# Shorter inverse roots, mixer B's key and value tiles in banks of three tags, and its first head four filling steps later

## The chip, the cores and the metric

The kernel runs on one core of one Trainium2 chip. The metric is the device time of one execution in microseconds (us). In the profile PE is the matrix engine (TensorE), PEld its weight loads, DVE the vector engine (VectorE), ACT the scalar engine (ScalarE), POOL is GpSimd, and SP is the engine that issues most of the DMAs (SyncE). A matmul's result goes to one of eight PSUM banks of 128 × 512 numbers.

## What is computed

Two layers of a trunk over 512 positions of width 1024, in float32. Each layer has two attention mixers side by side, gates that merge them, and then a channel mixer. Cut to what matters here:

```
h = rms_norm(x)
z = h @ W_in                # columns for mixer A, for its indexer, for mixer B, for two gates
# mixer A: indexer scores, the 128 best keys of each query (top-k), attention over these, 8 heads
# mixer B: latents, 8 heads of 64 + 32 numbers
cq   = rms_norm(cq);  qb = cq @ w_uq     # 384 -> 8 x 96, rotary on the last 32
ckv  = rms_norm(ckv); kv = ckv @ w_ukv   # 256 -> 8 x (64 key + 64 value)
kb   = concat(kv[..., :64], rope(kr))    # kr: 32 numbers that all heads share
qb, kb = rms_norm(qb), rms_norm(kb)      # over the 96 numbers of a head
y_b  = softmax(mask(qb @ kb.T * scale)) @ kv[..., 64:]
x = x + (sigmoid(ga) * (y_a @ w_a) + sigmoid(gb) * (y_b @ w_b)) @ w_out
x = x + down(silu(gate) * val)           # [gate, val] = conv3(rms_norm(x) @ w_up)
```

Every rms_norm needs an inverse square root of a mean of squares per position (or per position and head).

## The kernel before, in words

**Products.** [...] A product is then three matmuls: high × high, high × low, low × high. ScalarE copies out the high part, VectorE subtracts it from the source to make the low part (`split_into`, lines 312–319: the low part is due one tick after the high part). For weights the same is done ahead of their use (`Weights.split`), for some of them by a DMA that adds on GpSimd's queue (line 211).

**Order of the work.** The program is written as generators. `mix_dense` (line 572 on) is the *filling*: the dense columns of the input projection (line 535), mixer B's key, value and query tiles, mixer A's query, key and value rows (line 558). One filling step is the work up to its next `yield`: for dense columns three matmuls of 512 columns. A `Feeder` called `each_b` goes between the steps of mixer B's heads, and each call gives 0.85 filling steps while the first two heads run (`RATE_B`), and 0.2 steps of the top-k. The top-k (`top_k`, lines 1036 and 1043) is VectorE work: sixteen rounds of three maxima and three match-replaces over 512, 384 and 256 columns. It is handed out between filling steps, one operation per step while mixer B's first group of heads is made (`RATE_0`, line 1258). `later(n, f)` puts off `f` by n ticks. From what is so written the scheduler of the framework makes a fixed order of the instructions of each engine; each engine then runs its own queue in that order and waits at its head for whatever the instruction needs.

**PSUM.** The eight banks are handed out by tag: two of D (dense), three of L, two of T (mostly transposes), one of Y (line 277). A new tile of a tag takes the bank of the tile that many of its tag before, and its first matmul waits until that one's readers are done.

**Mixer B's tiles.** `attn_b(g)` (from line 833 on) makes heads 4g to 4g + 3. For each of the four blocks of 128 positions a key/value tile is made: six matmuls of 512 columns (line 856). Its bank is read by ScalarE (line 862, keys into `kn`; line 314, the values' high part into `vb`; line 843, squares into `sqb`) and by VectorE (line 315, the values' low part); line 844 sums the squares on VectorE into `ssk`. Three ticks later `keys()` adds to them the sum of squares of the shared rotary key `sskr` (line 870), makes the mean (line 871), the inverse root, and 22 ticks later scales the keys (`kn`, lines 879–880 on VectorE, the rotary part on GpSimd). Then four query tiles: nine matmuls of 384 columns each (line 893); ScalarE copies them out into `qn` (line 899), GpSimd turns them (lines 906–912), and `queries()` scales them (line 924, VectorE). All of these tiles have tag L (`BB`, line 97).

**The heads.** Before mixer B's first head `each_b` is called `GAP_B` = 12 times (line 1290). `turn_b` transposes a head's queries and keys (line 1149, into banks T) and splits them, `scores_b` makes its four rows of scores (lines 1164–1166, three matmuls each in a bank L), VectorE takes the maxima, ScalarE the exponentials (line 369), `softmax_end` scales them (lines 1056–1063), and `values` transposes the weights (line 1074) and multiplies (line 1081, bank Y). The scores of a head, the values of the head before and the transposes of the next go in turn, with `each_b` between.

**The inverse root** (`rsqrt`, line 343) is on VectorE: a first guess from the bits (line 346) and three Newton steps of three operations (lines 355–357), ten in a chain, on 4 or 16 numbers per partition. It is used by `Norm.finish` (line 485, then a copy in line 486), for the latents, for mixer A's heads, and in `keys()` and `queries()`.

Of the kernel before, what the change touches and what calls it, by code (L numbers as in the profile page):

```python
# [15 lines left out]
OP = mybir.AluOpType  # L16
AX = mybir.AxisListType
# [7 lines left out]
EPS = 1e-6  # L25
# [17 lines left out]
RATE_T = 0.2  # L43
LAG_S = 22
LAG_T = 4
GAP_B = 12
NORM_ACT = [3]
E_V = [2, 1, 2, 2, 2, 0]
PT = 0
# [29 lines left out]
LAG_D = [2, 4, 5, 7, 8, 10, 12]  # L79
WPOOL = []  # L80
WMOD = 1
NEWT = 1
WB = [4, 4, 3]
ENDS = 20
SPARE = (1, 3, 5)
# [9 lines left out]
GAP_I = 4  # L95
GAP_A = 12
BB = 'L'
LAG_N = 16
LAG_Q = 6
PSUM = {'D': 2, 'L': 3, 'T': 2, 'Y': 1}  # L100
# [146 lines left out]
def trunk(ctx: ExitStack, tc: tile.TileContext, xT, wd, vecs, bias, rot_n, outT):  # L247
# [92 lines left out]
        mm(p, lhsT=ah, rhs=bl, start=False, stop=False, skip_group_check=True)  # L340
        mm(p, lhsT=al, rhs=bh, start=False, stop=stop, skip_group_check=True)

    def rsqrt(a, shape, quick=False):

        y, t = small("y", shape), small("t", shape)
        V.tensor_scalar(y.bitcast(I32), a.bitcast(I32), -0.5, float(0x5F3759DF), op0=OP.mult, op1=OP.add)
        if not (quick or NEWT):
            for _ in range(3):
                G.tensor_tensor(out=t, in0=y, in1=y, op=OP.mult)
                G.tensor_tensor(out=t, in0=t, in1=a, op=OP.mult)  # L350
                G.tensor_scalar(t, t, -0.5, 1.5, op0=OP.mult, op1=OP.add)
                G.tensor_tensor(out=y, in0=y, in1=t, op=OP.mult)
            return y
        for _ in range(3):
            V.tensor_tensor(out=t, in0=y, in1=y, op=OP.mult)
            V.scalar_tensor_tensor(t, t, -0.5, a, op0=OP.mult, op1=OP.mult)
            V.scalar_tensor_tensor(y, t, 1.5, y, op0=OP.add, op1=OP.mult)
        return y

    def pin(ins, i, k):  # L360
        if i == 0 and k in PINS:
# [89 lines left out]
    class Norm:  # L451
# [17 lines left out]
        def finish(self, gap, turned):  # L469

            p = bank("T")
            v = small("v", [4])
            for i in range(4):
                c = slice(i * 128, (i + 1) * 128)
                if turned:
                    pin(nc.tensor.transpose(p[:, c], self.acc[:, c], ident), i, "F")
                else:
                    pin(mm(p[:, i:i + 1], lhsT=self.acc[:, c], rhs=ones[:, 0:1], start=True, stop=True), i, "F")
            if turned:
                V.tensor_reduce(out=v, in_=p.rearrange("p (t c) -> p t c", c=128), axis=AX.X, op=OP.add)  # L480
            total = v if turned else p[:, 0:4]
            self.epsv = cst.tile([128, 4], F32, name=nm("epsv"))
            self.rstd = cst.tile([128, 4], F32, name=nm("rstd"))
            V.tensor_scalar(v, total, 1.0 / D, EPS, op0=OP.mult, op1=OP.add)
            r = rsqrt(v, [4], quick=True)
            V.tensor_copy(self.rstd, r)
            V.tensor_scalar(self.epsv, v, EPS, None, op0=OP.mult)
            self.row = slot("row")

            def rest():  # L490
                self.spread(self.rstd, self.row)
                for f in self.waiting:
                    f()
                self.waiting = None
            later(gap, rest)
# [72 lines left out]
    st = {}  # L568
# [3 lines left out]
    def mix_dense(l, nrm):  # L572
# [23 lines left out]
        def turn_wk(wk):  # L596
# [33 lines left out]
            G.tensor_tensor(out=k3, in0=k3, in1=nrm.rstd[:, :, None].to_broadcast([128, 4, 32]), op=OP.mult)  # L630
            G.tensor_tensor(out=t3, in0=k3, in1=k3, op=OP.mult)
            ss = cst.tile([128, 4], F32, name=nm("sskr"))
            later(6, lambda: V.tensor_reduce(out=ss, in_=t3, axis=AX.X, op=OP.add))
            st["kr"], st["sskr"] = k3, ss

        raw, sqs = [], []
# [196 lines left out]
        def attn_b(g):  # L833
# [14 lines left out]
            h, o = W.get("kv", g)  # L848
            for t in range(4):
                ts = slice(t * 128, (t + 1) * 128)  # L850
                p = bank(BB)
                xs = [(st["ckvh"][k][:, ts], st["ckvl"][k][:, ts]) for k in range(2)]
                seq = ([(x, h, k) for k in range(2) for x in xs[k]] + [(xs[k][0], o, k) for k in range(2)] if "k" in LO
                       else [q for k in range(2) for q in ((xs[k][0], h, k), (xs[k][1], h, k), (xs[k][0], o, k))])
# [12 lines left out]

            def keys():
                m = small("mk", [4, 4])
                V.tensor_tensor(out=m, in0=ssk, in1=st["sskr"][:, :, None].to_broadcast([128, 4, 4]), op=OP.add)  # L870
                V.tensor_scalar(m, m, 1.0 / 96, EPS, op0=OP.mult, op1=OP.add)
                r = rsqrt(m, [4, 4])

                def scale():
# [776 lines left out]
```

## Time and profile before

| | |
|---|---|
| time, median of 3 runs | 1536.77 us (1535.88 to 1537.1) |
| the profiled execution | 1536.24 us, span 1534.5 us from its first to its last instruction |
| granted TensorE clock | 1.00 of full speed over the whole span |
| TensorE busy | 1525.7 us |
| VectorE busy | 1124.4 us |
| ScalarE busy | 946.3 us |
| GpSimd busy | 396.3 us |
| mixer B's key, value and query tiles and first heads | about 90 to 136 us in layer 0, 853 to 900 us in layer 1 |

A row of the time line is: start in us, duration in us, engine, line, operation, the tile written and the tiles read (numbers left out), for a matmul its rows and columns, then partitions × elements; in brackets how long the engine was idle before it and what ended that. Durations of one engine's instructions overlap: the next starts before the last part of the one before is written, so what one costs its queue is the distance of starts, which the prediction uses.

### The profile page before, as it was taken

Reading aid. Unit: us, or ns where it says so; the run is one execution under the profiler, and the core shown is the slowest. Engines: PE = TensorE matmul, PEld = TensorE weight load, DVE = VectorE, ACT = ScalarE, POOL = GpSimd, SP = SyncE. Lnnn points to the kernel's source line nnn. Section 1 sums busy time; section 2 is a strip of 40 time slices with the busy share of each in tenths; the row PEclk is TensorE's granted clock in tenths of the full one; section 3 lists DMA queues with packets and bytes.
Section 4 is the critical chain, followed back from the end, with each engine's and each line's share of the span. In section 5 each row is a group of like instructions: output and inputs, shape, how many; then the busy total and the mean of one; then the engine's idle time right before and its main releaser. Section 6 shows DMA issues by size and latency. Waiting matters only on the chain.

```text
span 1534.5 us, 23946 instructions
## 1 busy us (share of the span) xinstructions
PE 1525.7 (99%) x8658; PEld 1335.7 (87%) x8658; DVE 1124.4 (73%) x2305; ACT 946.3 (62%) x1553; POOL 396.3 (26%) x578
## 2 busy tenths in 40 slices
PE   9999999999999999999999999999999999999999
PEld 8887999888888898889998889998888888988899
DVE  7899988666476693547979999886674857835586
ACT  7756668773577536664557576687635765456642
POOL 2343012400011442124602520223001115311364
PEclk9999999999999999999999999999999999999999
DMA  7464124733488438873454641356436783488732
GB/s 247 108 158 119 53 86 113 190 118 116 128 191 190 104 117 218 194 177 90 152 171 112 159 107 56 104 134 174 129 97 147 182 189 91 149 197 197 181 99 91
DMA packets 73575, 216.29 MB, mean 141 GB/s; under 512 B 8432, under 2 KB 11504, under 8 KB 73456
## 3 DMA queue, kind: packets, MB, share of 16 engines
q1 hardware_dynamic: 54592, 149.08, 30.7%
q0 software_dynamic: 18432, 65.28, 22.8%
q8 instruction: 68, 1.11, 0.3%
q14 instruction: 51, 0.42, 0.1%
q10 hardware_dynamic: 432, 0.40, 0.1%
HBM read 141.06 MB, written 4.19 MB: 95 GB/s over the span
## 4 chain that ended last, share of the span: by engine, by line
PE 86%; DVE 11%; ACT 2%; issue 1%; DMA 0%; SPq 0%; DVEq 0%; ACTq 0%
PE D L535 37%; PE T L535 15%; PE D L558 7%; PE L L1446 5%; PE T L1446 4%; PE D L1446 3%; DVE sc L1043 2%; PE Y L1081 2%; DVE m L1036 2%; PE Y L1446 2%; PE T L1074 2%; PE L L535 2%; PE L L336 1%; PE L L335 1%; PE L L728 1%
## 5 line engine op out<-in xcount | busy, mean ns | idle before, releaser
L182 ACT CAST wh<-wr 128x1024 fp32r<-128x1024 f32 (+2 forms) x205 | 211.3, 1034 | 163.7 <-PE D L535 73.8
L211 POOL DMA_DIRECT2D wl<-wr x128 | 110.7, 874 | 630.2 <-ACT wl L210 591.9
L535 PE MATMUL D<-hxh,wh 128*128 128x512 f32 (+1 forms) x440 | 174.0, 396 | 0.0
L535 PE MATMUL D<-hxl,wh 128*128 128x512 f32 (+1 forms) x440 | 172.8, 393 | 0.0
L210 ACT ACTIVATE wl<-wr 128x1024 fp32r<-128x1024 f32 (+2 forms) x128 | 132.2, 1035 | 48.1 <-PE D L535 25.9
L200 ACT CAST wh<-wr 128x896 fp32r<-128x896 f32 x88 | 82.6, 942 | 102.4 <-POOL wr L224 56.2
L1115 POOL TENSOR_TENSOR P<-M,sel 128x128 f32<-128x128 f32 (+1 forms) x64 | 53.4, 889 | 271.2 <-DMA M<-in_bias_dram 150.2
L535 PE MATMUL D<-hxh,wl 128*128 128x512 f32 (+1 forms) x440 | 117.8, 393 | 0.0
L224 POOL TENSOR_TENSOR wr<-wr 128x256 f32<-128x256 f32 x88 | 101.0, 1151 | 57.9 <-DVE wr L223 41.9
L558 PE MATMUL D<-wh,hxh 128*128 128x256 f32 x384 | 113.8, 297 | 0.0
L205 DVE TENSOR_TENSOR wl<-wr,wh 128x896 fp32r<-128x896 f32 x88 | 101.9, 1161 | 10.2 <-ACT wh L200 4.3
L558 PE MATMUL D<-wl,hxh 128*128 128x256 f32 x384 | 109.3, 285 | 0.0
L558 PE MATMUL D<-wh,hxl 128*128 128x256 f32 x384 | 108.4, 283 | 0.0
L535 PE MATMUL D<-hrl,wh 128*128 128x512 f32 x256 | 99.6, 389 | 0.0
L535 PE MATMUL D<-hrh,wh 128*128 128x512 f32 x256 | 99.6, 389 | 0.0
L535 PE MATMUL T<-hrh,wh 128*128 128x512 f32 x256 | 99.6, 389 | 0.0
L535 PE MATMUL T<-hrl,wh 128*128 128x512 f32 x256 | 99.6, 389 | 0.0
L194 DVE TENSOR_TENSOR wl<-wr,wh 128x1024 fp32r<-128x1024 f32 x77 | 94.9, 1238 | 6.3 <-ACT wh L182 5.6
L535 PEld LDWEIGHTS D<-hxh,wh 128*128 128x128 f32 x440 | 82.9, 188 | 13.4 <-DVE gb L702 0.2
L535 PEld LDWEIGHTS D<-hxl,wh 128*128 128x128 f32 x440 | 82.9, 188 | 12.7
L535 PEld LDWEIGHTS D<-hxh,wl 128*128 128x128 f32 x440 | 80.2, 188 | 14.0
L1390 DVE SCALAR_TENSOR_TENSOR c<-T,vec,c 128x511 f32<-128x511 f32 x32 | 23.9, 748 | 89.1 <-ACT c L1387 89.1
(458 smaller groups left out, 4571.4 us busy)
## 6 DMA issues: line engine op xcount, KB each, us to landing
wr<-in_wd_dram SPq DMA_DIRECT2D x197, 512.0 KB, 3.8
wl<-wr POOLq DMA_DIRECT2D x120, 512.0 KB, 5.4
wr<-in_wd_dram SPq DMA_DIRECT2D x88, 256.0 KB, 2.6
x<-in_xT_dram SPq DMA_DIRECT2D x16, 256.0 KB, 5.2
M<-in_bias_dram SPq DMA_DIRECT2D x16, 256.0 KB, 4.0
wr<-in_wd_dram SPq DMA_DIRECT2D x7, 384.0 KB, 3.2
kah<-kah SPq DMA_DIRECT2D x16, 128.0 KB, 4.3
kal<-kal SPq DMA_DIRECT2D x16, 128.0 KB, 3.8
```

The source lines that it names most:

```text
L182: ins = self.nc.scalar.copy(h[:, :n], t[:, :n])
L194: eng.tensor_tensor(out=o[:, c], in0=t[:, c], in1=h[:, c].bitcast(F32), op=OP.subtract)
L200: self.nc.scalar.copy(h[:, :896], t[:, 128:1024])
L205: self.later(lag, lambda: self.nc.vector.tensor_tensor(out=o[:, :896], in0=t[:, 128:1024], in1=h[:, :896].bitcast(F32), op=OP.subtract))
L210: self.nc.scalar.activation(o, t, AF.Copy, scale=-1.0)
L211: self.nc.gpsimd.dma_start(o.bitcast(F32), t, accum_op=OP.add)
L224: g(2)(out=b[:, 6:8], in0=b[:, 0:3:2], in1=b[:, 3:6:2], op=OP.add)
L535: mm(p[:, t0:], lhsT=w, rhs=x[:, t0:], start=n == 0, stop=n == len(seq) - 1, skip_group_check=True)
L558: mm(pp[b][:, t, :], lhsT=x, rhs=w, start=n == 0 and half == 0 and t == 0, stop=n == 11 and half == 1, skip_group_check=True)
L1036: ins = V.max(out=m8[i], in_=st["sc"][i][:, :128 * (i + 1)])
L1115: G.tensor_tensor(out=P[:, P0[i]:P0[i] + w], in0=M[:, 512 - w:512], in1=sel[:, SEL0[i]:SEL0[i] + w], op=OP.add)
L1446: mm(p, lhsT=w, rhs=x, start=b0, stop=b1, skip_group_check=True)
```

## The change

Three things are done. The inverse root has a Newton step and then one step of third order, 1 + 3 + 4 = 8 operations instead of 10, and can write straight into its destination, so that `Norm.finish` needs no copy; the branches that were never taken go. In the keys' root the mean and EPS are put into one operation with the addition, and for that `sskr` is scaled beforehand by one small operation on GpSimd, behind VectorE's sum of line 633. The key/value tiles take their banks from `KV_BANKS`: L, Y, T, T for group 0 and Y, T, L, L for group 1, while the query tiles stay with L. And `GAP_B` goes from 12 to 16.

```diff
-GAP_B = 12
+GAP_B = 16
-NEWT = 1
+CUBE = 0.375 ** 0.5
 BB = 'L'
+KV_BANKS = ('LYTT', 'YTLL')
...
-    def rsqrt(a, shape, quick=False):
+    def rsqrt(a, shape, out=None):
         y, t = small("y", shape), small("t", shape)
         V.tensor_scalar(y.bitcast(I32), a.bitcast(I32), -0.5, float(0x5F3759DF), op0=OP.mult, op1=OP.add)
...
-        for _ in range(3):
-            V.tensor_tensor(out=t, in0=y, in1=y, op=OP.mult)
-            V.scalar_tensor_tensor(t, t, -0.5, a, op0=OP.mult, op1=OP.mult)
-            V.scalar_tensor_tensor(y, t, 1.5, y, op0=OP.add, op1=OP.mult)
-        return y
+        V.tensor_tensor(out=t, in0=y, in1=y, op=OP.mult)
+        V.scalar_tensor_tensor(t, t, -0.5, a, op0=OP.mult, op1=OP.mult)
+        V.scalar_tensor_tensor(y, t, 1.5, y, op0=OP.add, op1=OP.mult)
+        V.tensor_tensor(out=t, in0=y, in1=y, op=OP.mult)
+        V.scalar_tensor_tensor(t, t, -CUBE, a, op0=OP.mult, op1=OP.mult)
+        V.scalar_tensor_tensor(t, t, 1.25 / CUBE, t, op0=OP.add, op1=OP.mult)
+        V.scalar_tensor_tensor(y if out is None else out, t, 1.875, y, op0=OP.add, op1=OP.mult)
+        return y if out is None else out
...
-            r = rsqrt(v, [4], quick=True)
-            V.tensor_copy(self.rstd, r)
+            rsqrt(v, [4], self.rstd)
...
-            later(6, lambda: V.tensor_reduce(out=ss, in_=t3, axis=AX.X, op=OP.add))
+            def key_sums():
+                V.tensor_reduce(out=ss, in_=t3, axis=AX.X, op=OP.add)
+                G.tensor_scalar(ss, ss, 1.0 / 96, EPS, op0=OP.mult, op1=OP.add)
+            later(6, key_sums)
...
-                p = bank(BB)
+                p = bank(KV_BANKS[g][t])
...
-                V.tensor_tensor(out=m, in0=ssk, in1=st["sskr"][:, :, None].to_broadcast([128, 4, 4]), op=OP.add)
-                V.tensor_scalar(m, m, 1.0 / 96, EPS, op0=OP.mult, op1=OP.add)
+                V.scalar_tensor_tensor(m, ssk, 1.0 / 96, st["sskr"][:, :, None].to_broadcast([128, 4, 4]),
+                                       op0=OP.mult, op1=OP.add)
```

The instructions of TensorE are the same in number; VectorE has 52 fewer, GpSimd two more (one in each layer). The order of TensorE's instructions differs only from mixer B's tiles to the start of mixer A, in both layers alike. Two places in layer 0 show it. A row is line, operation, the tile written, the tiles read, and the size; a number behind a name tells tiles of one name apart. In the changed kernel lines 312 to 345 have numbers higher by one, the dense columns' line 535 is 531, line 558 is 554, and the lines from 640 on are the same.

VectorE, where group 1's value copies stand, before: `vb` are the values (lines 315, 316 after), `mq` and `y`, `t` belong to the queries' root of group 0, `ssk` to the keys of group 1, `kn` are group 0's keys.

```order
L315 TENSOR_TENSOR vb_1266<-L_1272,vb_1266 128x4x64
L918 SCALAR_TENSOR_TENSOR mq_1290<-ssq_1066,ms_952 128x16
L880 TENSOR_TENSOR kn_1053<-kn_1053,y_1167 128x4x64
L346 TENSOR_SCALAR y_1292<-mq_1290 128x16
L315 TENSOR_TENSOR vb_1267<-L_1286,vb_1267 128x4x64
L355 TENSOR_TENSOR t_1293<-y_1292 128x16
L844 TENSOR_REDUCE ssk_1270<-sqb_1283 128x4
L356 SCALAR_TENSOR_TENSOR t_1293<-t_1293,mq_1290 128x16
L844 TENSOR_REDUCE ssk_1270<-sqb_1310 128x4
L357 SCALAR_TENSOR_TENSOR y_1292<-t_1293,y_1292 128x16
L315 TENSOR_TENSOR vb_1268<-L_1313,vb_1268 128x4x64
```

The same place of VectorE's queue in the changed kernel, from group 1's first value copy to its third:

```order
L316 TENSOR_TENSOR vb_1259<-Y_1265,vb_1259 128x4x64
L918 SCALAR_TENSOR_TENSOR mq_1283<-ssq_1062,ms_948 128x16
L1036 MAX m_165_871<-sc_555 128x8
L347 TENSOR_SCALAR y_1285<-mq_1283 128x16
L316 TENSOR_TENSOR vb_1260<-T_1279,vb_1260 128x4x64
L348 TENSOR_TENSOR t_1286<-y_1285 128x16
L844 TENSOR_REDUCE ssk_1263<-sqb_1276 128x4
L349 SCALAR_TENSOR_TENSOR t_1286<-t_1286,mq_1283 128x16
L844 TENSOR_REDUCE ssk_1263<-sqb_1301 128x4
L350 SCALAR_TENSOR_TENSOR y_1285<-t_1286,y_1285 128x16
L316 TENSOR_TENSOR vb_1261<-L_1304,vb_1261 128x4x64
```

The copies read banks of Y, T and L in place of L alone. The key scaling that stood between the first two is gone from there (all four stand ahead of the first copy now; before, three stood behind the third), and a 512-wide maximum of the top-k has come in.

TensorE, where head 0's queries and keys are transposed, before: `qn` are group 0's queries, `kn` its keys, `D` a dense tile of the filling.

```order
L535 MATMUL D_1560<-hxl_175,wh_1237 128x512
L535 MATMUL D_1560<-hxh_182,wh_1237 128x512
L1149 MATMUL T_1429<-ident,qn_1057 100x128
L1149 MATMUL T_1452<-ident,kn_1053 100x128
L1149 MATMUL T_1452<-ident,kn_1054 100x128
L1149 MATMUL T_1429<-ident,qn_1058 100x128
L1149 MATMUL T_1452<-ident,kn_1055 100x128
L1149 MATMUL T_1452<-ident,kn_1056 100x128
L535 MATMUL D_1560<-hxl_183,wh_1237 128x512
L1149 MATMUL T_1429<-ident,qn_1059 100x128
```

The same transposes in the changed kernel; `L_1395` is the third and `L_1464` the fourth query tile of group 1.

```order
L893 MATMUL L_1395<-wl_1117,cqh_774 128x384
L893 MATMUL L_1395<-wl_1226,cqh_865 128x384
L1149 MATMUL T_1455<-ident,qn_1053 100x128
L1149 MATMUL T_1455<-ident,qn_1054 100x128
L893 MATMUL L_1464<-wh_1116,cqh_680 128x384
L1149 MATMUL T_1455<-ident,qn_1055 100x128
L893 MATMUL L_1464<-wh_1116,cql_681 128x384
L893 MATMUL L_1464<-wh_1116,cqh_774 128x384
L893 MATMUL L_1464<-wh_1116,cql_775 128x384
```

Before, the third and fourth query tile stood behind these transposes, in between head 0's scores; now they stand ahead of and around them, and the dense matmuls that stood there (16 in a row) follow behind the transposes, ahead of head 0's first scores.

More of the change, by code (lines that the diff above doesn't have):

```diff
@@ L341, in mm3 @@
         mm(p, lhsT=al, rhs=bh, start=False, stop=stop, skip_group_check=True)
-    def rsqrt(a, shape, quick=False):
+    def rsqrt(a, shape, out=None):
         y, t = small("y", shape), small("t", shape)
         V.tensor_scalar(y.bitcast(I32), a.bitcast(I32), -0.5, float(0x5F3759DF), op0=OP.mult, op1=OP.add)
-        if not (quick or NEWT):
-            for _ in range(3):
[L349 to L352, printed above, removed]
-            return y
-        for _ in range(3):
-            V.tensor_tensor(out=t, in0=y, in1=y, op=OP.mult)
-            V.scalar_tensor_tensor(t, t, -0.5, a, op0=OP.mult, op1=OP.mult)
-            V.scalar_tensor_tensor(y, t, 1.5, y, op0=OP.add, op1=OP.mult)
-        return y
+        V.tensor_tensor(out=t, in0=y, in1=y, op=OP.mult)
[6 more added lines that the diff above has]
+        return y if out is None else out
     def pin(ins, i, k):
```

## The prediction

> **What bounds the kernel now.** The page comes first.
>
> ```profile
> span 1534.5 us, 23946 instructions
> PE 1525.7 (99%) x8658; PEld 1335.7 (87%) x8658; DVE 1124.4 (73%) x2305; ACT 946.3 (62%) x1553; POOL 396.3 (26%) x578
> PE 86%; DVE 11%; ACT 2%; issue 1%; DMA 0%; SPq 0%; DVEq 0%; ACTq 0%
> ```
>
> TensorE is busy for 99% of the span, yet the chain that ended last is VectorE for 11% of it: there are stretches in which TensorE's queue stands behind VectorE. The change keeps the count of TensorE's instructions, so only such waits can be won. Busy times by stretch show where they are: the columns are the length, then busy time of PE, PEld, DVE, ACT and POOL, the granted clock, the DMA share and GB/s.
>
> ```profile
> core 0: us, PE busy (x) PEld busy (x) DVE busy (x) ACT busy (x) POOL busy (x), PEclk, DMA share, GB/s
> 30.00:36.00 6.00, 6.00 (x31) 4.95 (x30) 5.10 (x17) 2.00 (x3) 0.00 (x0) 1.00 0.78 251
> 90.00:113.00 23.00, 21.74 (x103) 18.07 (x103) 23.00 (x82) 17.38 (x41) 13.91 (x44) 1.00 0.70 172
> 113.00:136.00 23.00, 22.23 (x119) 17.38 (x118) 22.74 (x74) 16.41 (x37) 14.46 (x35) 1.00 0.57 134
> 853.00:877.00 24.00, 23.57 (x114) 20.04 (x112) 24.00 (x84) 18.73 (x44) 15.25 (x47) 1.00 0.72 178
> ```
>
> In mixer B's key, value and query tiles (90 to 113 us, and 853 to 877 in layer 1) VectorE has no idle time at all and TensorE has some. TensorE's time line of layer 0 shows the waits (start, duration, instruction, and in brackets the idle time and its releaser).
>
> ```profile
> 90.27 0.39 PE L856 MATMUL L<-wh,ckvh 128*128 128x512 f32 x1
> 91.63 0.39 PE L856 MATMUL L<-wh,ckvh 128*128 128x512 f32 x1
> ...
> 94.72 0.50 PE L856 MATMUL L<-wh,ckvh 128*128 128x512 f32 x1 [0.21 <-DVE vb L315]
> ...
> 100.19 0.44 PE L893 MATMUL L<-wh,cqh 128*128 128x384 f32 x1 [0.46 <-DVE vb L315]
> ...
> 108.94 0.50 PE L856 MATMUL L<-wh,ckvh 128*128 128x512 f32 x1 [0.59 <-DVE vb L315]
> ...
> 110.43 0.33 PE L893 MATMUL L<-wh,cqh 128*128 128x384 f32 x1
> ...
> 115.23 0.32 PE L1149 MATMUL T<-ident,qn 128*100 128x128 f32 x1
> ...
> 117.26 0.32 PE L1149 MATMUL T<-ident,qn 128*100 128x128 f32 x1
> ...
> 119.26 0.60 PE L1149 MATMUL T<-ident,qn 128*100 128x128 f32 x4
> 119.61 0.32 PE L1164 MATMUL L<-tbh,tbh 100*128 100x128 f32 x1
> ...
> 131.83 0.39 PE L535 MATMUL D<-hxl,wh 128*128 128x512 f32 x1
> 132.78 0.50 PE L1164 MATMUL L<-tbh,tbh 100*128 100x512 f32 x1 [0.57 <-ACT P L369]
> ```
>
> Each wait of lines 856 and 893 is for a bank of tag L, which VectorE's copy of the values' low part (line 315) gives back. A key/value tile of six matmuls takes 91.63 − 90.27 = 1.36 us when nothing waits, one 512-column matmul 1.36/6 = 0.227. The same in layer 1:
>
> ```profile
> 853.84 0.39 PE L856 MATMUL L<-wh,ckvh 128*128 128x512 f32 x1
> 859.28 0.33 PE L893 MATMUL L<-wh,cqh 128*128 128x384 f32 x1
> 860.86 0.33 PE L893 MATMUL L<-wh,cqh 128*128 128x384 f32 x1
> ...
> 871.33 0.50 PE L856 MATMUL L<-wh,ckvh 128*128 128x512 f32 x1 [0.43 <-DVE vb L315]
> 872.82 0.33 PE L893 MATMUL L<-wh,cqh 128*128 128x384 f32 x1
> ...
> 894.80 0.84 PE L535 MATMUL D<-hxh,wl 128*128 128x512 f32 x3
> 896.08 0.33 PE L1074 MATMUL T<-ident,P 128*128 128x128 f32 x1 [0.44 <-DVE P L1063]
> ```
>
> A query tile takes 860.86 − 859.28 = 1.58. So the eight key/value tiles and group 0's four query tiles need 8 × 1.36 + 4 × 1.58 = 17.2 us. In layer 0 they took 110.43 − 90.27 = 20.16, of which two dense matmuls are 0.45: 2.5 us of stall. In layer 1 872.82 − 853.84 = 18.98, three dense matmuls among it (0.68): 1.1 us. In layer 0 group 0's four query transposes at 115.23 to 117.26 come (117.26 − 115.23)/3 = 0.68 apart, VectorE's pace of scaling. By the order seven transposes, at (119.61 − 119.26)/4 = 0.09, and three dense matmuls fill 1.3 of these 2.03 us; so an estimated 0.6 is lost there, with the time to restart left out. Head 0's last score row waits 132.78 − 131.83 − 0.23 = 0.72, and in layer 1 its transpose 896.08 − 894.80 − 3 × 0.227 = 0.6.
>
> **The banks, layer 0.** With the change a key/value tile no longer waits for the tile three before it: the ring of L holds only two such tiles per group. Waits remain for the two query tiles of group 1 that take over the banks of its last two key/value tiles. Unhindered, TensorE comes to the first of them, the second query tile of group 1, at 90.27 + 8 × 1.36 + 5 × 1.58 = 109.0. It needs VectorE's third value copy of group 1. What that copy is behind is priced by these VectorE rows.
>
> ```profile
> 99.26 0.54 DVE L1043 MATCH_REPLACE8 sc<-m,sc 128x384 f32<-128x384 f32 x1
> 99.72 0.41 DVE L315 TENSOR_TENSOR vb<-L,vb 128x256 fp32r<-128x256 f32 x1
> ...
> 101.71 0.55 DVE L1036 MAX8 m<-sc 128x8 f32<-128x384 f32 x1
> 102.18 0.17 DVE L346 TENSOR_SCALAR y<-mk 128x16 int32<-128x16 int32 x1
> 102.27 0.41 DVE L1036 MAX8 m<-sc 128x8 f32<-128x256 f32 x1
> ...
> 110.79 0.41 DVE L315 TENSOR_TENSOR vb<-L,vb 128x256 fp32r<-128x256 f32 x1
> ...
> 112.06 0.41 DVE L880 TENSOR_TENSOR kn<-kn,y 128x256 f32<-128x256 f32 x1
> 112.39 0.16 DVE L355 TENSOR_TENSOR t<-y 128x16 f32<-128x16 f32 x1
> ...
> 113.97 0.41 DVE L315 TENSOR_TENSOR vb<-L,vb 128x256 fp32r<-128x256 f32 x1
> ```
>
> A 384-wide match-replace holds the queue for 99.72 − 99.26 = 0.46, a 384-wide maximum for 0.47, a key scaling for 0.33, and a 16-element step between others for 102.27 − 102.18 = 0.09. By the new order the stretch up to that copy starts 0.46 − 2 × 0.10 = 0.26 later (one match-replace more ahead, two fewer steps in the latents' root), has one match-replace and one maximum fewer (−0.93), three key scalings more (+1.0) and three small steps fewer (−0.27): +0.06. The copy starts at 110.85 instead of 110.79, and gives its bank back 0.41 later, at 111.26. TensorE waits 2.2. The fourth copy then follows after three scalings and one small step fewer but a maximum more, 113.97 − 110.79 − 0.6 = 2.6 later, at 113.4, free at 113.85; the third query tile comes to it at 111.3 + 1.58 + two dense matmuls (0.45) = 113.4 with a restart of 0.1, and waits 0.45. With two restarts that makes 2.9 in place of 2.5 + 0.6 = 3.1: the transposes now stand behind the third query tile, when the scalings are done. Gain 0.2 to 0.3; the bounds are a change of −2.5 (banks free in time) and +0.5 (one more operation of 0.47 ahead of the copy).
>
> **The banks, layer 1.** VectorE is less far behind there.
>
> ```profile
> 873.22 0.41 DVE L315 TENSOR_TENSOR vb<-L,vb 128x256 fp32r<-128x256 f32 x1
> ```
>
> TensorE would come to the waiting tile at 853.84 + 10.88 + 7.9 + 0.45 = 873.1, the bank is free at 873.22 + 0.41 + 0.06 = 873.7: 0.55 of wait, as much again at the third tile and at the transposes that now come soon after. That is 1.1 to 1.6 against 1.1 and the waits behind it: gain 0; the bounds are a change of −1.1 (all of the stall goes) and +0.5 (the upper of these two).
>
> **The head later.** Four filling steps more at a rate of 0.85 are 3.4 steps, up to ten 512-column matmuls (10 × 0.227 = 2.3 us), that now stand ahead of head 0's scores; the query tiles are no longer between its scores. The softmax chain of head 0 gets that as cover: the 0.72 and 0.6 above go. Gain 1.3; bounds 0 and 1.3.
>
> **The root in eight operations.** VectorE issues 52 operations fewer (22 roots by two, four copies, four in the keys' mean). Alone in a chain such a step costs 0.20:
>
> ```profile
> 33.03 0.16 DVE L355 TENSOR_TENSOR t<-y 128x4 f32<-128x4 f32 x1
> 33.23 0.16 DVE L356 SCALAR_TENSOR_TENSOR t<-t,v 128x4 f32<-128x4 f32 x1
> ```
>
> So 52 × 0.09 to 52 × 0.20 = 4.7 to 10.4 us of VectorE. That between 90 and 113 us is in the sum above; the rest is hidden: the norm's root around 33 us has TensorE busy with dense columns for 6.00 of 6.00 us. Without that cover the four norms would give 4 × 3 × 0.20 = 2.4. Value taken 0. [...]
>
> **The key sums on GpSimd.** Its new 4-element operation stands ahead of a DMA issue.
>
> ```profile
> 43.98 1.06 POOL L211 DMA_DIRECT2D wl<-wr  x1 [1.16 <-ACT wl L210]
> ```
>
> That issue waited 1.16 us for ScalarE anyway; the operation is off the path, 0. If it came after ScalarE, it would delay the issue by less than that.
>
> **The sum.** 0.25 + 0 + 1.3 + 0 = 1.6 us. The profiled execution took 1536.24 (span 1534.5 and 1.7 around it), the median is 1536.77, 0.53 above: 1534.6 for a profiled one, 1535.2 for the median. 0.2% is 3.07 us, about what can be told from no change.
>
> **The rivals.** (1) VectorE's lag comes from the banks: its copies are late only since TensorE's tiles are. For it: VectorE's copies alternate with TensorE's waits all through 94 to 109. Against it: VectorE is busy for 23.00 of 23.00 us. Then all stalls go: 2.5 + 0.6 in layer 0, 1.1 in layer 1 and the 1.3 at the heads, 5.5, less the restarts of some 0.1 that a bank change costs here and there, 0.5: 5.0, so 1531.8. [...]
> (2) No net gain: head 0's waits return at head 1, since VectorE must still do the top-k rounds. Gain 0.2 to −0.5: 1536.6 to 1537.3.
> (3) Slower: the matmuls put ahead are missing behind. Filling that stood between the later heads stands ahead of the first now; the last heads' softmax chains then run uncovered by up to 2.3 us in each layer. Without the 1.3 that is 4.6 − 0.3 = 4.3 slower: 1541.1. It decides against the bound from (3.07 + 0.3)/2 = 1.7 per layer. Against it: the new order still has three to six dense matmuls between nearly all the rows of scores of the later heads.
>
> **The numbers.** The forecast 55%, its own range 1533.6 to 1536.5; rival 1 27%, rival 2 12%, rival 3 6%. The range goes from rival 1's time, 1531.8, to rival 2's end, 1537.3; outside are rival 3 and what goes past rival 1's full price. Faster by over 0.2% (below 1533.7): rival 1 and the forecast's edge, 0.30; slower: rival 3, 0.06; within: 0.64.
>
> **What would show it.** Right: no L856 row behind a value copy; L893 rows of group 1 that wait near 2.2 and 0.45 behind the copy in layer 0, each about 0.5 in layer 1; head 0's first scores unhindered; VectorE still full from 90 to 113. Rival 1 shows the second query tile of group 1 starting at 109 to 109.5. Rival 3 shows new idle time on TensorE in the heads after the fifth. The mechanism is wrong if the third value copy starts before 110 or the waits lie elsewhere.

## The result

The changed kernel took 1544.9 us (median of 6 runs, 1543.8 to 1546.5) against 1536.3 (5 runs, 1535.9 to 1537.1) of the kernel before on the same chip: a ratio of 1.0056 [1.0042, 1.0070], or 8.6 us slower. A sixth run of the kernel before, a slow one, took 8666 us and is left out here. The profiled execution took 1544.33 us. The first lines of its page:

```profile
span 1542.6 us, 23897 instructions
PE 1527.7 (99%) x8658; PEld 1338.5 (87%) x8658; DVE 1124.7 (73%) x2253; ACT 946.4 (61%) x1553; POOL 387.7 (25%) x580
PE 88%; DVE 9%; ACT 2%; issue 1%; ACTq 0%
```

The span grew by 8.1 us, TensorE's busy time by only 2.0, and VectorE's did not fall although 52 operations are gone. Where the 8.1 lie is read from two rows per layer: TensorE's first matmul of mixer B's tiles and its last one of mixer A's projected rows. After:

```profile
90.63 0.39 PE L856 MATMUL L<-wh,ckvh 128*128 128x512 f32 x1
269.09 0.28 PE L554 MATMUL D<-wl,hxh 128*128 128x256 f32 x1
...
1035.35 0.28 PE L554 MATMUL D<-wl,hxh 128*128 128x256 f32 x1
```

The same last matmuls before (the first ones stand in the prediction):

```profile
265.75 0.28 PE L558 MATMUL D<-wl,hxh 128*128 128x256 f32 x1
...
1027.22 0.28 PE L558 MATMUL D<-wl,hxh 128*128 128x256 f32 x1
```

In layer 0 this stretch took 178.46 us, before 175.48: +3.0; in layer 1 (from 857.19, below) 178.16 against 173.38, +4.8. That is 7.8 of the 8.1. Within a stretch TensorE's order differs between the kernels, so stages are compared by their *excess*: for each TensorE instruction the distance to the next start, less the median of that distance for the same instruction in the kernel before, added up (worked out from the trace's rows). Tiles means from the first key/value tile through the first two heads; later, from there to the end of mixer A's rows, with heads 3 to 8 of mixer B and the first of mixer A in it.

| excess, us | tiles, layer 0 | later, layer 0 | tiles, layer 1 | later, layer 1 | elsewhere |
|---|---|---|---|---|---|
| before | 5.4 | 3.3 | 3.1 | 3.5 | 6.6 |
| after | 5.6 | 6.1 | 5.5 | 5.8 | 7.0 |

Three places lost, then: the later heads of both layers (2.8 and 2.3) and the tiles of layer 1 (2.4). First the tiles. TensorE's waits after, in layer 0 and, from 857 on, in layer 1:

```profile
112.23 0.69 PE L893 MATMUL L<-wh,cqh 128*128 128x384 f32 x1 [2.66 <-DVE vb L316]
...
857.19 0.39 PE L856 MATMUL L<-wh,ckvh 128*128 128x512 f32 x1
...
877.99 0.45 PE L893 MATMUL L<-wh,cqh 128*128 128x384 f32 x1 [1.86 <-DVE vb L316]
880.89 0.45 PE L893 MATMUL L<-wh,cqh 128*128 128x384 f32 x1 [0.60 <-DVE vb L316]
```

No key/value tile waits any more, and the second query tile of group 1 does, as foretold: 2.66 us in layer 0. In layer 1 it waits 1.86, and the third 0.60. What the long wait does besides is in the granted clock (the third column from the right):

```profile
core 0: us, PE busy (x) PEld busy (x) DVE busy (x) ACT busy (x) POOL busy (x), PEclk, DMA share, GB/s
90.00:113.00 23.00, 20.34 (x99) 17.98 (x98) 23.00 (x76) 18.40 (x44) 15.22 (x49) 0.98 0.67 162
...
112.00:113.00 1.00, 0.77 (x2) 0.77 (x3) 1.00 (x5) 0.00 (x0) 1.00 (x6) 0.60 1.11 221
113.00:114.00 1.00, 1.00 (x5) 1.00 (x5) 1.00 (x6) 0.00 (x0) 1.00 (x6) 0.50 1.05 205
...
115.00:116.00 1.00, 1.00 (x5) 0.90 (x4) 1.00 (x4) 0.48 (x2) 0.00 (x0) 0.70 1.04 188
116.00:117.00 1.00, 1.00 (x8) 1.00 (x7) 1.00 (x4) 0.39 (x1) 0.93 (x2) 1.00 0.74 295
```

For 3.4 us, from 112.2 to 115.6, TensorE has half its clock (0.50) and issues five matmuls per us instead of eight or more: an estimated 1.6 us, by which "busy" TensorE grew. Now layer 1's third value copy, by VectorE's rows:

```profile
874.90 1.25 DVE L880 TENSOR_TENSOR kn<-kn,y 128x256 f32<-128x256 f32 x1
...
877.52 0.41 DVE L316 TENSOR_TENSOR vb<-L,vb 128x256 fp32r<-128x256 f32 x1
```

A key scaling that took 0.41 us in the prediction takes 1.25 here. GpSimd at that time:

```profile
874.61 0.57 POOL L908 TENSOR_TENSOR qn<-qn,rotn 128x64 f32<-128x64 f32 x1
...
875.17 0.64 POOL L876 TENSOR_TENSOR kn<-kr,y 128x128 f32<-128x128 f32 x1
875.53 0.79 POOL L910 TENSOR_TENSOR qn<-qn,rot 128x64 f32<-128x64 f32 x1
```

GpSimd's operations follow one another without a gap past 876.32, and VectorE's scaling, begun at 874.90 among them, ends at 876.15. The copy comes 877.52 − 857.19 = 20.33 us after the first tile, against 873.22 − 853.84 = 19.38 before. Last the later heads of layer 0. Everything that TensorE waited for between 185 and 275 us, before and after (total us, times, longest):

```profile
PE T L1149 <- DVE qao L329: 0.2, 1, 0.2
PE T L1074 <- DVE kal L804: 0.2, 1, 0.2
```

```profile
PE T L1074 <- DVE kal L804: 0.6, 1, 0.6
PE Y L1081 <- DVE ptl L316: 0.6, 1, 0.6
PE T L1074 <- DVE qao L330: 0.2, 1, 0.2
PE D L554 <- DVE va L319: 0.2, 1, 0.2
```

Layer 1 shows the same four waits of 0.6, 0.6, 0.2 and 0.2, so they go with the order of the instructions. Together they are 1.6 us a layer, against 0.4 before; the rest of the 2.8 lies in shorter gaps that are not followed here. The first: mixer A's key transposes (line 793) each hold a T bank until VectorE has read it twice (line 804), and they now come close together:

```profile
208.69 0.63 PE L793 MATMUL T<-ident,raw 128*128 128x128 f32 x4
210.44 0.62 PE L793 MATMUL T<-ident,raw 128*128 128x128 f32 x4
215.61 0.63 PE L1074 MATMUL T<-ident,P 128*128 128x128 f32 x4 [0.58 <-DVE kal L804]
```

Before, they started at 208.98 and 213.59 with value transposes between them. The second is at mixer A's first head (VectorE, then GpSimd, then TensorE):

```profile
257.79 1.09 DVE L347 TENSOR_SCALAR y<-m 128x16 int32<-128x16 int32 x1
...
260.16 0.69 DVE L316 TENSOR_TENSOR ptl<-T,pth 128x512 fp32r<-128x512 f32 x1
```

```profile
255.78 3.06 POOL L1115 TENSOR_TENSOR P<-M,sel 128x128 f32<-128x128 f32 x4 [8.10 <-PE T L1074]
```

```profile
260.90 0.50 PE L1081 MATMUL Y<-ptl,va 128*128 128x512 f32 x1 [0.56 <-DVE ptl L316]
```

A step on 16 numbers, first of a root, stands 1.09 us instead of 0.17 while GpSimd adds mixer A's mask to the selection: it ends at 258.88, GpSimd at 258.84. Before, that step ran at 255.00, ahead of GpSimd's 255.69, in 0.17. But the kernel before has a held step too, a later step of the same root:

```profile
256.71 0.68 DVE L315 TENSOR_TENSOR ptl<-T,pth 128x512 fp32r<-128x512 f32 x1
...
257.69 1.09 DVE L357 SCALAR_TENSOR_TENSOR y<-t,y 128x16 f32<-128x16 f32 x1
```

There `ptl` goes ahead of the held step, here it stands behind it: the order decides who pays.

### The profile page after: what moved, and what is told of

It reads as the page before. It is cut to its first block, busy times and chain, and to the rows that moved or that the text cites. A ratio compares the mean times of both kernels' runs of the same rounds, so it can differ in the third digit from the quotient of the medians.

```text
span 1542.6 us, 23897 instructions
## 1 busy us (share of the span) xinstructions
PE 1527.7 (99%) x8658; PEld 1338.5 (87%) x8658; DVE 1124.7 (73%) x2253; ACT 946.4 (61%) x1553; POOL 387.7 (25%) x580
## 4 chain that ended last, share of the span: by engine, by line
PE 88%; DVE 9%; ACT 2%; issue 1%; ACTq 0%
PE D L531 40%; PE T L531 15%; PE L L1446 5%; PE D L554 5%; PE T L1446 4%; PE D L1446 3%; PE Y L1081 2%; PE Y L1446 2%; PE L L531 2%; PE T L1074 2%; DVE sc L1043 1%; DVE m L1036 1%; PE L L337 1%; PE L L336 1%; PE L L728 1%
## 5 line engine op out<-in xcount | busy, mean ns | idle before, releaser
L225 POOL TENSOR_TENSOR wr<-wr 128x256 f32<-128x256 f32 x88 | 93.5, 1065 | 63.9 <-DVE wr L224 55.4
```

The costliest lines, as they stand in the source:

```text
L225: g(2)(out=b[:, 6:8], in0=b[:, 0:3:2], in1=b[:, 3:6:2], op=OP.add)
```

## The experiments

Three theories were set against each other. *The order*: the time is made by which of VectorE's works come ahead of what TensorE needs, and each part of the change disturbs an order that fitted. *The clock*: the waits themselves are as foretold, and the lost clock behind them costs. *The lock*: a VectorE operation on SBUF tiles is held up beside GpSimd's, as the key scaling above was (1.25 us instead of 0.41), so a price from a quiet place is too low. Ratios are against the kernel before on the same chip, with 95% intervals.

### One part at a time

**The head alone**: `GAP_B = 16` in the kernel before.

> The kernel before with GAP_B 16 alone. Theory 'later head' (the four filling steps taken ahead of head 0 put the last query tiles ahead of the transposes and are missing behind, where transposes and value products of the last heads then wait for VectorE): 4 to 6 us slower than before, with the excess of TensorE between the third head of mixer B and the end of mixer A's rows about 2.4 us larger in each layer, as in the changed kernel. Theory 'gathered wait' (the banks gather the waits of the tiles into one, after which the granted clock is low for some us): within 1 us of before here, and no stretch below a clock of 1.00.

1542.5 us, 1.0036 [1.0024, 1.0049]. The excess is 4.7 and 3.5 at the tiles, 6.9 and 5.6 later. So the gain foretold at the first heads of layer 0 is there (0.7), and 3.6 and 2.2 are paid later. The head alone costs 5.5 us, where all three parts together cost 8.6.

**The banks alone**:

```diff
-                p = bank(BB)
+                p = bank(KV_BANKS[g][t])
```

> The kernel before with the bank tags L, Y, T, T and Y, T, L, L alone. Theory 'gathered wait': one wait of over 2 us at the second query tile of group 1 in layer 0, the granted clock below 1.00 behind it, 1.5 to 3 us slower than before. Theory 'later head': within 1 us of before, the last heads' waits as before.

1539.2 us, 1.0015 [1.0006, 1.0024]. The eleven executions fall into groups: five took 1537.7 to 1538.0 us (0.7 to 1.0 above the kernel before) at a mean granted clock of 1.000, two, also at 1.000, 1539.2 and 1539.7, and four 1540.7 to 1541.2 at 0.998 or 0.999. The trace is of one of the last four. Most of its loss is in layer 1's tiles (6.1 against 3.1). VectorE there, then TensorE:

```profile
872.54 1.86 DVE L919 SCALAR_TENSOR_TENSOR mq<-ssq,ms 128x16 f32<-128x16 f32 x1
```

```profile
876.57 0.62 PE L894 MATMUL L<-wh,cqh 128*128 128x384 f32 x1 [2.38 <-DVE vb L316]
```

Sixteen numbers per partition in 1.86 us, beside GpSimd's rotations of queries and keys (from 872.06 to 874.36 without a break); before, that operation took 0.16. The value copy behind it is late, and TensorE waits 2.38 us, with half clock from about 876.7 to 880. The theory of the lock fits this, at a place to which the new order brought the operation.

**The roots alone**, with the mean in one operation, `GAP_B = 12` and all tiles in L.

> The kernel before with the root in eight operations and the fused keys' mean alone. Both theories: no slower than before, 0 to 1.5 us faster, since VectorE has less to do and it is what the tiles wait for. A theory that the new root is itself the cost (a longer way through the queue at some place) has it slower by over 2 us.

1540.2 us, 1.0023 [1.0014, 1.0032]. Less work for VectorE, and slower by 3.2 to 3.5. All four key scalings now stand ahead of group 1's first value copy, and TensorE's wait there goes from 0.59 to 1.09.

**Roots and banks, `GAP_B = 12`**, and **roots and head, all tiles in L**:

> The changed kernel with GAP_B back at 12. Theory 'later head': back to the time of before or up to 2 us faster, no excess in the last heads. Theory 'gathered wait': the wait at the second query tile of group 1 in layer 0 stays over 2 us, the granted clock falls behind it, 1.5 to 3 us slower than before.

> The changed kernel with all tiles in banks of tag L again. If the three parts add up: 3 us below the changed kernel, about 1541.5. If the banks cost only through the long wait that the other parts lengthen: 4 us below.

1541.8 us, 1.0028 [1.0016, 1.0040], and 1544.7 us, 1.0048 [1.0036, 1.0061]. The later part of the first is like that of the kernel before (4.0 and 3.5), that of the second like the changed kernel's (6.2 and 5.6). So the later loss comes with the head. The parts don't add up: alone they cost 5.5, 2.3 and 3.2, together 8.6 and not 11.0.

### How far the head is moved

The kernel before with `GAP_B` = 20 and = 8:

> The kernel before with GAP_B 20, four steps more again. Theory 'filling is missing behind' (what is put ahead lacks later): the loss of the first four steps is paid twice, 9 to 12 us slower than before. Theory 'phase' (the last heads' transposes meet the transposes of mixer A's keys in the two banks T, which depends on how the filling lies against the heads): not in proportion, between 1 us faster and 6 us slower than before.

> The kernel before with GAP_B 8. Theory 'filling is missing behind': four steps fewer ahead are four more behind, the excess behind head 2's first scores is at or below before's (3.3 and 3.5 us), and what is lost is in the tile stage. Theory 'phase': the excess behind is larger in spite of more filling.

1552.4 us, 1.0107 [1.0093, 1.0121], and 1547.4 us, 1.0063 [1.0049, 1.0077]. Excess of the later part: 8.0 and 8.7 with 20, 6.9 and 7.8 with 8, where 12 has 3.3 and 3.5. If filling put ahead were simply missing behind, 8 would be as good as 12 or better there. It is not, so where the filling falls against VectorE's and GpSimd's work counts as well. The 15.8 us of 20 lie above what either theory gave; there TensorE also waits 2.13 and 2.04 us at head 0's transposes, with 6.8 and 3.4 us at half clock behind. With 8, TensorE waits at mixer A's key bank again, but the two transposes are 4.7 us apart; so their closeness goes with 16 and is not the cause in general.

**Giving the steps back**: `GAP_B = 16`, and `RATE_B[0]` 0.73 in place of 0.85, so that by the third head as much filling has been handed out as before.

> The kernel before with GAP_B 16 and the rate of filling during the first two heads lowered from 0.85 to 0.73, which gives the steps taken ahead back by head 2. Theory 'filling is missing behind': the excess behind head 2's first scores falls from 6.9 and 5.6 us (GAP_B 16 alone) to near 3.3 to 4.5 in each layer, 2 to 4 us faster than GAP_B 16 alone (1542.5). Rival (the loss comes from the order in the first two heads itself): no faster than GAP_B 16 alone.

1540.0 us, 1.0013 [1.0004, 1.0022]: 1.8 us above the kernel before on its chip, where the head alone stood 5.5 above it (later part 4.9 and 4.8). This fits a part of the loss being filling that is missing behind. VectorE at mixer A's first head is then ahead of GpSimd, which starts at 257.41:

```profile
256.53 0.17 DVE L346 TENSOR_SCALAR y<-m 128x16 int32<-128x16 int32 x1
```

The wait behind `ptl` is gone there; waits for `kal` and `qao` (0.4 and 0.5) remain.

### The copies brought forward

The top-k from its tenth round on is held behind group 1's third value copy, in the changed kernel and in the one before:

```diff
...
+                c = copies.get((st["l_"], 1), [])
+                if rnd >= HOLD and len(c) > WHICH:
+                    tc.add_manual_dep(ins.ins, c[WHICH].ins.name, no_sync, reason="top k behind the copies")
```

> The changed kernel with the top-k from its tenth round on held back until group 1's third value copy. Theory 'VectorE's queue' (what stands ahead of the copies in VectorE's order makes the long wait, and the operations saved by the shorter root were filled up with others): the third copy of group 1 starts at least 3 us earlier in both layers, TensorE waits under 0.5 us at the second query tile, the clock stays at 1.00, 4 to 7 us faster than the changed kernel unless the top-k that is put off makes waits later. Rival 'chain' (the copies are late through their own chain of ScalarE and matmuls): the copy moves by under 1 us.

> The kernel before with the same hold. Theory 'VectorE's queue': the waits of the key/value tiles (2.5 and 1.1 us) go but for restarts, 1.5 to 3.5 us faster than before. Rival 'banks' (three banks L are too few whatever VectorE does): under 1 us of these waits goes. If the put-off top-k is late for others: no faster, with new waits behind 115 us.

1546.8 us, 1.0066 [1.0053, 1.0080], and 1539.4 us, 1.0020 [1.0011, 1.0029]. In the changed kernel the third copy comes 17.47 us after the first tile in layer 0, not 21.14, and the wait of 2.66 goes. It turns up again at head 0's transposes (VectorE, GpSimd, TensorE):

```profile
115.19 2.62 DVE L351 SCALAR_TENSOR_TENSOR t<-t,mk 128x16 f32<-128x16 f32 x1
...
118.83 0.68 DVE L318 TENSOR_TENSOR tbl<-T,tbh 100x512 fp32r<-100x512 f32 x1
```

```profile
115.37 0.46 POOL L915 TENSOR_TENSOR qn<-qn,rot 128x64 f32<-128x64 f32 x1
```

```profile
119.56 0.43 PE L1157 MATMUL T<-ident,qn 128*100 128x128 f32 x2 [2.55 <-DVE tbl L318]
```

Again 16 numbers take 2.62 us, to 117.81, while GpSimd's operations go on one behind the other to 117.86. Layer 1 has the same wait, of 2.30 us, and half clock behind it. In the kernel before, the hold takes away layer 0's waits (excess 4.2 instead of 5.4), and the top-k that is put off costs more later (4.9 and 6.0).

### The clock

Twelve more matmuls of 128 columns, whose results nobody reads, ahead of group 1's first query tile, to break the long wait:

```diff
...
+                for n in range(EXTRA if g == 1 and t == 0 else 0):
+                    mm(p[:, 384:512], lhsT=xs[0][0], rhs=tiles[0][0][:, 0:128], start=n == 0, stop=n == EXTRA - 1,
+                       skip_group_check=True)
```

> The changed kernel with twelve extra matmuls of 128 columns, whose result nobody reads, ahead of group 1's first query tile, so that TensorE idles less at the second. Theory 'clock' (an idle of more than 2 us halves the granted clock for some 3.3 us, which costs 1.6 us on top of the wait): the idle in layer 0 falls to some 1.5 us, no stretch at 0.50 there, and the time is 1 to 3 us below the changed kernel's. Rival (the wait alone costs, and the clock costs nothing): within 0.7 us of the changed kernel.

1549.4 us, 1.0085 [1.0071, 1.0099]. The wait in layer 0 falls into 1.36 and 1.75 and the clock stays 1.00 there, but the added matmuls delay what VectorE's queue waits for, and TensorE waits a further 1.54 at head 0's transposes; in layer 1 a wait of 2.24 has half clock behind it. It doesn't price the clock, and the 1.6 us stay an estimate from the spacing of the matmuls.

The single executions of roots and banks (`GAP_B = 12`) bear it out. Two with a mean granted clock of 1.000 took 1539.6 and 1540.2 us, one with 0.999 took 1541.0, and three with 0.998 took 1542.6 to 1543.7. The trace is of one of these three and has two stretches of 3.41 us at half clock, which take 0.002 off the mean; the difference of 3.3 us is 1.6 for each. This is a correlation: what else differs between the executions isn't on record, and one of the head alone lists 0.949 without being longer (1542.6).

### GpSimd's rotations

Without the six operations that turn mixer B's queries (lines 906 to 911): the queries go on unturned. TensorE's and VectorE's orders stay the same.

> The changed kernel without GpSimd's six operations of the queries' rotation (that part of the computation is left out); the orders of TensorE and VectorE stay as they are. Theory 'lock' (VectorE's operations with two inputs in SBUF stand still while GpSimd's operations run, and so the value copies come late): the key scalings of 0.62 to 1.25 us fall to 0.41, the third copy of group 1 comes 0.5 us (layer 0) and 1 us or more (layer 1) sooner after the start of the tiles, the waits of the second query tile shrink by as much, and the time is 2 to 4 us below the changed kernel's. Theory 'queue' (only the count of operations ahead decides): under 1 us.

> The kernel before without GpSimd's rotation of the queries (left out), the reference for the two beside it. By the lock theory some 0.5 to 2 us faster than before, since its own small VectorE operations are stretched less than the changed kernel's.

> The shorter roots and fused mean alone, without GpSimd's rotation of the queries (left out). Theory 'lock': what made the roots alone 3 us slower was that the key scalings came to lie beside GpSimd's rotations, so without these the kernel with the new roots is no slower than the kernel before without them (0 to 2 us faster), and the tile stage's excess is at or below that kernel's. Theory 'order' (the scalings stand ahead of the value copies, whatever GpSimd does): still 1 to 3 us slower than the kernel before without the rotations.

> Roots and banks with GAP_B 12, without GpSimd's rotation of the queries (left out). Theory 'lock': the roots and the banks were the gain that was forecast once the value copies are on time: 1 to 3 us faster than the kernel before without the rotations, no stretch below a clock of 1.00. Theory 'banks' (the gathered wait costs in any case): 1 to 3 us slower than that kernel.

| without rotation | us | ratio | tiles, layers 0, 1 | later, layers 0, 1 |
|---|---|---|---|---|
| the kernel before | 1533.2 | 0.9971 [0.9960, 0.9982] | 3.2, 1.5 | 3.6, 3.4 |
| roots alone | 1536.3 | 0.9994 [0.9985, 1.0002] | 3.9, 2.8 | 4.3, 4.6 |
| roots and banks | 1536.2 | 0.9989 [0.9980, 0.9999] | 3.8, 2.7 | 4.4, 3.6 |
| the changed kernel | 1539.3 | 1.0006 [0.9998, 1.0015] | 4.2, 2.3 | 5.9, 5.7 |

In layer 1 of the changed kernel without rotations, VectorE and TensorE:

```profile
873.11 0.41 DVE L880 TENSOR_TENSOR kn<-kn,y 128x256 f32<-128x256 f32 x1
...
874.76 0.41 DVE L316 TENSOR_TENSOR vb<-L,vb 128x256 fp32r<-128x256 f32 x1
```

```profile
875.23 0.44 PE L893 MATMUL L<-wh,cqh 128*128 128x384 f32 x1 [0.37 <-DVE vb L316]
```

The scaling takes 0.41, and the wait is 0.37 where 0.55 was foretold and 1.86 stood. So the rotations explain two thirds of what layer 1's tiles lost: 2.4 us with them (5.5 against 3.1), 0.8 without (2.3 against 1.5). Without rotations the queries are also ready earlier, which the times don't separate from the lock; the scaling's own 0.41 instead of 1.25 is the lock's mark. Two things it does not explain. The later heads are as bad without rotations (5.9 and 5.7); the mask's addition on GpSimd, line 1115, was left in, so the lock's share there isn't priced. And the roots still cost 3.0 us against the kernel before without rotations, roots and banks 2.9, where the lock had both at or below it: for them the order stands and the lock falls. In all the rotations make the change worse by 2.5 us by the medians (8.6 − 6.1), 3.2 by the ratios, whose intervals leave some 3 either way.

**Six memsets in place of the rotation** (the queries again unturned):

> The changed kernel with the six operations of the queries' rotation replaced by six that set a scratch tile of the same size to zero (the rotation is left out, GpSimd stays busy, but those operations read nothing). Theory 'lock on reading': VectorE as in the kernel without them, 2 to 4 us below the changed kernel. Theory 'lock on any GpSimd operation': VectorE's operations as slow as in the changed kernel, within 1 us of it.

1547.7 us, 1.0062 [1.0048, 1.0075], for a reason not foreseen: the memsets wait for nothing, and GpSimd ran them at the program's start. At the tiles the kernel is like the one without rotations (3.7 and 2.3); the loss is ahead of them, for the first key/value tile starts at 100.12 us instead of 90.63. TensorE waits 7.22 us there for a cast and then has half clock up to 18.2. VectorE at that place, and the same cast in the changed kernel:

```profile
4.12 7.72 DVE L1206 CAST wh<-w 128x256 fp32r<-128x256 f32 x1 [2.94 <-DMA w<-in_wd_dram]
```

```profile
4.01 0.29 DVE L1206 CAST wh<-w 128x256 fp32r<-128x256 f32 x1 [2.82 <-DMA w<-in_wd_dram]
```

From 3.49 to 12.00 us GpSimd worked through the 96 memsets of 0.14 us, one behind the other, and the cast took 7.72 us instead of 0.29. It ends at 11.85, beside the last two memsets, the only ones that take over 0.2 us:

```profile
11.67 0.27 POOL L910 MEMSET rot<- 128x64 f32 x1
11.76 0.24 POOL L911 MEMSET rot<- 128x64 f32 x1
```

**The rotation in four operations instead of six**, on twice as many numbers at a time, in the kernel before and in the changed one:

```diff
...
-                    G.tensor_tensor(out=x1, in0=x1, in1=b(cos), op=OP.mult)
-                    G.tensor_tensor(out=x2, in0=x2, in1=b(cos), op=OP.mult)
+                    G.tensor_tensor(out=x, in0=x, in1=b(cos), op=OP.mult)
...
```

> The kernel before with GpSimd's rotation of the queries in four operations of 128, 128, 64 and 64 columns in place of six of 64 (the same computation; the orders of TensorE and VectorE stay word for word). Without the rotations at all the kernel before was 3.7 us faster. Theory 'lock' (GpSimd's time beside VectorE is what costs): about 1.36 us of GpSimd per tile in place of 1.68, a fifth less, so 0.3 to 1.5 us faster than before. Rival (the rotation costs as a dependence, by when it ends): under 0.3 us.

> The changed kernel with the same four operations. Theory 'lock': its key scalings in layer 1 shrink (1.25 and 0.87 us), the idle of the second query tile there falls below 1.86 us, 0.5 to 2 us faster than the changed kernel, still slower than before by 6 us or more. Rival: within 0.5 us of the changed kernel.

1536.7 us, 0.9994 [0.9985, 1.0003], and 1544.4 us, 1.0043 [1.0030, 1.0056]. Both medians point the lock's way, neither beyond the intervals. Layer 1's rows of the changed kernel do not: the scaling takes 1.42 us instead of 1.25, beside fewer but longer operations of GpSimd, and the wait is 1.95, not below 1.86. No version that computes the same was found that beats the kernel before beyond the interval.

## Why the prediction was wrong

**The head later** is the step that failed: "the 0.72 and 0.6 above go. Gain 1.3; bounds 0 and 1.3". The lower bound left out a loss, which stood only as the third rival and was given 6% on the ground that three to six dense matmuls stayed between the later scores. The 0.72 in layer 0 did go; in layer 1 the wait of 0.6 moved to head 0's scores (0.68, behind `tbl`). But the heads from the third on lost 2.8 and 2.3 us. The rival had the place and the order of the price (up to 2.3 per layer, 1541.1 in all; the head alone took 1542.5), but only a part of the cause: giving the steps back made the kernel faster, yet with 8 steps instead of 16 the same stretch loses as much or more (6.9 and 7.8 against 6.9 and 5.6). The waits that were found, 1.6 us a layer, are at single places where VectorE's work for mixer A now falls beside a full pair of T banks or beside GpSimd; the rest of the loss there stays open.

**The banks, layer 0** came out by its mechanism: the third copy 111.77 − 90.63 = 21.14 us after the first tile where 20.58 was worked out, the wait 2.66 where 2.2 was. What was missing in the sum is the clock, an estimated 1.6, for which no row of before gave a price. Without it the excess would have been 4.0 against 5.4. The third tile's 0.45 did not come: at half clock the second tile took 3.05 us instead of 1.58 (112.23 to 115.28), and the bank was free by then.

**The banks, layer 1** failed by the price of a row: "the bank is free at 873.22 + 0.41 + 0.06 = 873.7". The order was moved so that key scalings stand beside GpSimd's rotations, and they were priced at 0.33 of queue time from a place where GpSimd was not in the way. The wait was 1.86, beyond the upper bound; without the rotations 0.37. The third tile's 0.55 was 0.60.

**The root in eight operations**: "Value taken 0" was too good by 3.2 to 3.5 us. The copies do not come earlier when VectorE has less to do, since its queue is in a fixed order, and the shorter chain made the scheduler put the scalings ahead of the copies. Without rotations 0.7 and 1.3 of it are at the tiles; why the later part grows too (0.7 and 1.2) isn't settled.

**The key sums** show no cost of their own: the excess elsewhere is 7.0 against 6.6.

**Rival 1** (the banks were the shortage) fell: with more banks TensorE waits longer at fewer places. VectorE was full from 90 to 113 us before and after.

The lock stands in none of these sums, since no row that was taken as a price showed it. Three operations of VectorE took 1.86 us (banks alone), 2.62 (top-k held) and 7.72 (memsets) beside GpSimd's where 0.16 to 0.29 was due, and in these three cases VectorE did not get in between GpSimd's operations, one close behind the other, either. In the traces of the kernel before and of the changed one no operation of VectorE that reads a PSUM bank took more than 0.014 us over the median of its kind, while of those with SBUF tiles alone some took up to 1.08 and 1.20 over it (worked out from the traces' rows).

## What to carry to other kernels

Where engines run queues in a fixed order, an edit that shortens one chain or moves one start re-deals the whole order: compare what stands ahead of each operation that the busiest engine waits for, over all the stages that share the filling, and let a loss into the bounds of every such step. Price VectorE's operations from rows that had the same neighbour on GpSimd: a step on 16 numbers took 0.16 us here or 2.62, according to what GpSimd was at. And gather waits into one long one with care: here one of 2.66 us cost clock (0.50 for 3.4 us) as well as time.

## What was not expected of the hardware

**The clock after a wait.** After waits of TensorE between 1.7 and 2.7 us the granted clock was 0.50 for 3.4 us in some cases and 1.00 in others, and the length alone doesn't decide. Without rotations the changed kernel waited 1.74 us, and roots and banks 1.73; the first got half clock, the second not. TensorE of the changed kernel without rotations, then of roots and banks:

```profile
111.53 0.52 PE L893 MATMUL L<-wh,cqh 128*128 128x384 f32 x1 [1.74 <-DVE vb L316]
```

```profile
111.18 0.44 PE L893 MATMUL L<-wh,cqh 128*128 128x384 f32 x1 [1.73 <-DVE vb L316]
```

What differs is where the wait falls. In the changed kernel's trace the clock is 1.00 for 105.81 us, 0.50 for 3.41 and 1.00 for 1426.77: 31, 1 and 418 times 3.413. Stretches of that length around the two waits, in the two kernels (after the length TensorE's busy time; the clock is third from the right):

```profile
108.34:111.76 3.42, 1.69 (x10) 1.36 (x9) 3.42 (x15) 3.31 (x7) 2.67 (x9) 1.00 0.84 217
111.76:115.17 3.41, 3.41 (x11) 3.31 (x11) 3.41 (x13) 0.52 (x2) 0.00 (x0) 0.50 1.05 208
```

```profile
106.65:110.06 3.41, 2.80 (x15) 2.29 (x13) 3.41 (x11) 3.36 (x8) 2.67 (x9) 1.00 0.51 143
110.06:113.47 3.41, 2.29 (x12) 2.20 (x13) 3.41 (x15) 1.24 (x4) 1.19 (x3) 1.00 1.08 220
113.47:116.88 3.41, 3.33 (x20) 2.41 (x19) 3.41 (x14) 0.00 (x0) 0.00 (x0) 1.00 0.95 246
```

The first wait lies in one stretch, which is idle for 1.73 us, and the next stretch runs at half clock; the second is cut into 0.61 and 1.12, and nothing follows. The changed kernel itself has both cases. Its wait of 2.66 us leaves the stretch from 108.78 to 112.19 idle for 2.62, and half clock follows; its wait of 1.86 in layer 1 is cut into 0.65 and 1.21, and the clock stays 1.00:

```profile
108.78:112.19 3.41, 0.79 (x5) 0.46 (x3) 3.41 (x13) 2.63 (x7) 3.41 (x13) 1.00 0.95 246
112.19:115.61 3.42, 3.38 (x10) 3.38 (x11) 3.42 (x12) 0.10 (x1) 1.97 (x9) 0.50 1.06 207
873.36:876.78 3.42, 2.76 (x15) 2.25 (x13) 3.42 (x10) 3.42 (x9) 3.42 (x13) 1.00 0.91 156
876.78:880.19 3.41, 2.20 (x11) 1.87 (x11) 3.41 (x15) 1.62 (x5) 3.01 (x12) 1.00 1.03 263
880.19:883.60 3.41, 2.63 (x15) 2.25 (x15) 3.41 (x10) 1.38 (x4) 3.19 (x8) 1.00 0.84 210
```

Of the other stretches of that length in its trace and in that of the kernel before (worked out from the rows and the clock records), but for the last of each, in which the program ends, none is idle for more than 1.21 us, and 1.00 follows each of them. With the top-k held, the wait of 2.55 us, 1.72 of it in the fullest stretch, was not followed by half clock. Beyond these cases nothing is shown.

**GpSimd's run of operations as one lock.** An operation of VectorE stood not beside one operation of GpSimd but through several that followed each other, even a cast with one operand beside memsets (7.72 us). In three cases it got in about when the run ended: at 874.40 (banks alone, GpSimd's rotations to 874.36), 117.81 (GpSimd to 117.86) and 11.85 (to 12.00). Not always: layer 1's scaling in the changed kernel ended at 876.15 while GpSimd went on.
